# Output projection's second half tile by tile, with h kept in full for the FFN's combinations

## The chip, the cores and the metric

The kernel runs on one core of a Trainium2 chip. A time is the device time of one execution in microseconds (us). Five engines matter: TensorE (PE in the profile; PEld is its weight load, which overlaps it), VectorE (DVE), ScalarE (ACT), GpSimd (POOL), and SyncE (SP), whose queue issues most of the DMA transfers. Each engine takes its instructions in a fixed order; what waits at the head of an engine's or a queue's order holds all that stands behind it.

## The reference, cut to what matters

One decoder layer on x (1024 tokens by 1024 channels, float32): two attention branches are merged by gates, and then

```python
x = x + merged @ w_out                       # output projection
h2 = rms_norm(x, norm_ffn_g)
gu = h2 @ w_ffn_in                           # 1024 x 5632
x = x + (silu(gu[:, :2816]) * gu[:, 2816:]) @ w_ffn_down
return rms_norm(x, norm_final_g)
```

The change lies in the output projection, the norm behind it, and the first two of the 22 column blocks of the FFN's first product.

## The kernel before

**Precision.** Float32 products are made of three reduced ones. `split` (lines 98 to 100) turns a float32 tile into a high part, which ACT writes, and a low part, the difference, which DVE writes behind it. `mm3` (lines 102 to 105) then adds hi*hi, hi*lo and lo*hi into one PSUM bank: three matmuls for each block of 128 in the contraction, with names `wh` and `wl` for the two parts of a weight and `hT_t` for the two parts of the transposed activations.

**Buffers.** `load_w` (lines 110 to 129) brings a weight into one of two raw buffers `wr`, and splits it into one of two `wh`, `wl` pairs. The next load into a raw buffer is issued by SP when the splits have read it; the next split waits until PE has used the old pair. In the output projection the third and fourth quarter of the weight use pairs `wo` of their own, but the same two raw buffers. PSUM has six banks `pd` for products and two banks `pf`/`pt` for transposes and some products.

**The output projection** (lines 987 to 1027) goes over two halves of the 1024 output columns (`c0`). In each half, for the first 512 tokens (`hh == 0`, four tiles of 128 tokens) the contraction is the outer loop: for each of the eight blocks `k` all four tiles add three matmuls, 12 in all, and the weight quarters come in one by one. For the other four tiles (`hh == 1`) the tile is the outer loop: 24 matmuls a tile. Behind a tile, `take(t)` (lines 995 to 1000) adds the residual x on DVE. In the second half it also stores the row and calls `norm_transpose` (lines 167 to 180): ACT squares and sums the row, ACT and DVE make the scale, DVE writes the normed row `hn`, PE transposes it in two groups of four 128x128 blocks into the two banks `pt`, and `split` brings each bank to `hT_t`. With the contraction outside, the first four tiles of the second half end together.

**Beside it**, `right_side` (lines 976 to 985) loads two rows of blocks of `w_ffn_down` (1 MB) into one of three buffers `r`, makes four differences on POOL and stores them; eight of these run in the output projection, two in its first half.

**The seam to the FFN.** Two column blocks of the FFN are made plainly (`plain(0)`, `plain(1)`, lines 1049 to 1079), the others by a scheme with seven products for eight (`up`), which needs sums and differences of blocks of h2: T2, T3, T4 and T1. Between `plain(0)` and `plain(1)`, `back` adds hi and lo again to get each of the four blocks of h2 in float32 (four additions of 128x2048 on DVE), four more such operations make the combinations, and three splits write T3, T2 and T4.

**What sets the order.** A scheduler builds the order of each engine from the program with its own idea of durations; `tc.issue_after(i)` tells it to put an instruction behind i.

Of the kernel before, what the change touches and what calls it, by code (L numbers as in the profile page):

```python
# [15 lines left out]
P = 128  # L16
# [31 lines left out]
def layer_kernel(  # L48
# [49 lines left out]
    def split(hi, lo, src):  # L98
        last_hi[0] = nc.scalar.activation(out=hi, in_=src, func=AF.Copy)  # L99
        return nc.vector.tensor_tensor(out=lo, in0=src, in1=hi.bitcast(F32), op=ALU.subtract)  # L100
# [6 lines left out]
    last_mm, last_hi, last_sq = [None], [None], [None]  # L107
# [59 lines left out]
    def norm_transpose(xt, gain, hT, col, pool, by_sqrt, bufs=2):  # L167
# [7 lines left out]
        for k0 in range(0, KT, 4):  # L175
            pt = psf.tile([P, HALF], F32, tag="f", name=nm("pt"))
            for k in range(4):
                nc.tensor.transpose(pt[:, k * P:(k + 1) * P], hn[:, (k0 + k) * P:(k0 + k + 1) * P],
                                    ident[:])
# [790 lines left out]
    x1_dram = dpool.tile([NT, P, D], F32, name="x1_dram")  # L970
    x_ctx = pool_of("xpool", 1, side="right")
    x1 = x_ctx.__enter__().tile([P, NT, D], F32, name="x1")
    with pool_of("wout", 2) as mpool:
        gain2 = load_gain(mpool, norm_ffn_g)

        def right_side(n):
# [3 lines left out]
            nc.sync.dma_start(out=r[:].rearrange("p n b c -> p n (b c)"),  # L980
# [5 lines left out]

        for c0 in range(0, D, HALF):
            ws = []
            for hh in range(2):
# [5 lines left out]
                def take(t):  # L995
                    xs = x1[:, 4 * hh + t, c0:c0 + HALF]
                    nc.vector.tensor_tensor(out=xs, in0=pts[t][:], in1=xs, op=ALU.add)
                    if c0 > 0:
                        nc.scalar.dma_start(out=x1_dram[4 * hh + t], in_=x1[:, 4 * hh + t, :])
                        norm_transpose(x1[:, 4 * hh + t, :], gain2, hT[hh], t * P, mpool, True, 4)  # L1000

                if hh == 0:
                    for k in range(KT):
                        if k % 2 == 0:
                            src = w_out[k * P:(k + 2) * P, c0:c0 + HALF]
                            ws.append(load_w(src, 2, HALF) if k < 4 else
                                      load_w(src, 2, HALF, tag="wo", pool=mpool))
                            if c0 == 0:
                                with tc.issue_after(last_w[0].ins):
                                    last_w[0] = nc.sync.dma_start(  # L1010
                                        out=x1[:, k:k + 2, :], in_=x[k * P:(k + 2) * P, :].rearrange(
                                            "(t p) d -> p t d", p=P))
# [12 lines left out]
    x_ctx.__exit__(None, None, None)  # L1025


# [12 lines left out]
    k_ctx = pool_of("keep", 1, side="right")  # L1040
    f1 = k_ctx.__enter__().tile([P, 4, HALF], F32, name="f1")

    r_ctx = pool_of("odd", 2, side="right")
    rpool = r_ctx.__enter__()
# [4 lines left out]
    with pool_of("first", 2) as fpool:  # L1049

        def plain(j):
            sg = [fpool.tile([P, HALF], F32, tag="sg", name=nm("sg")) for _ in range(2)]
            a = fpool.tile([P, S], F32, tag="a", name=nm("a"))

            def evac_g(hh, pt):

                nc.scalar.activation(out=sg[hh][:], in_=pt[:], func=AF.Sigmoid)
# [308 lines left out]
```

## Time and profile before

| | |
|---|---|
| median of 3 runs | 1461.54 us (1459.87 to 1465.85) |
| the profiled execution | 1464.02 us, of which 1462.3 us are the profile's span |
| PE busy | 1439.0 us, 98% of the span |
| DVE, ACT, POOL busy | 956.4, 554.3, 505.1 us |
| output projection | about 707 to 797 us of the span |
| `plain(0)` and `plain(1)` | about 797 to 854 us |

A row of a timeline has the start, the length, the engine, the line, the operation with output and inputs, how many are merged into the row, and in brackets the idle time before it with what ended it. PE's lengths overlap, since matmuls are pipelined: its pace is read from start to start. A row of the table of windows has, for each engine, the busy us and the number of instructions, then the granted TensorE clock (PEclk), the busy share of the DMA engines, and GB/s.

### The profile page before, as it was taken

To read this page: it belongs to the slowest core of one execution; us is meant where nothing else is said; L and a number is where in the kernel's file an instruction comes from. 1 tells how busy PE (TensorE), PEld (TensorE's weight loads), DVE (VectorE), ACT (ScalarE), POOL (GpSimd) and SP (SyncE) were. 2 spreads that over 40 slices of the span, in tenths; PEclk is the share of its full clock that TensorE was granted. 3 is DMA by queue.
4 is the path that set the end of the run, shared out by engine and by line. 5 is a ranking of instruction groups with operands and counts; after the bars stand their busy time and mean duration, and the time that the engine had idled before them with its cause. 6 is when DMAs were issued, how large, how long until landed. Compare 5 with 4: busy or idle time off the path is not lost.

```text
span 1462.3 us, 18377 instructions
## 1 busy us (share of the span) xinstructions
PE 1439.0 (98%) x6876; PEld 1165.4 (80%) x6876; DVE 956.4 (65%) x1336; ACT 554.3 (38%) x824; POOL 505.1 (35%) x438
## 2 busy tenths in 40 slices
PE   8999999999999999999999999999999999999997
PEld 8898888877676776788887778888888888888886
DVE  6484654358889899936627874556665655765655
ACT  5333332236655523354315242322332223644333
POOL 1020444535533321110146176566666664100000
PEclk9999999999999999999999999999999999999999
DMA  8232454574543461275859322233332332966512
GB/s 232 73 101 79 145 165 122 138 215 125 135 115 110 152 223 37 73 236 162 306 201 336 122 75 72 90 105 108 108 109 97 105 115 101 353 252 231 186 47 85
DMA packets 165784, 213.58 MB, mean 146 GB/s; under 512 B 13760, under 2 KB 115136, under 8 KB 165440
## 3 DMA queue, kind: packets, MB, share of 16 engines
q1 hardware_dynamic: 129376, 119.06, 26.1%
q0 software_dynamic: 15344, 55.59, 10.7%
q10 hardware_dynamic: 20976, 37.76, 8.2%
q8 instruction: 54, 0.88, 0.2%
q14 instruction: 34, 0.28, 0.1%
HBM read 146.32 MB, written 66.06 MB: 145 GB/s over the span
## 4 chain that ended last, share of the span: by engine, by line
PE 87%; DVE 7%; issue 2%; POOL 2%; ACT 1%; DMA 1%; SPq 0%; ACTq 0%; DVEq 0%; POOLq 0%
PE pd L299 30%; PE pd L1281 10%; PE pf L299 7%; PE pd L103 7%; PE pd L104 6%; PE pd L105 6%; PE pf L104 3%; PE pf L105 3%; PE pf L103 3%; PE pd L711 1%; PE pd L197 1%; PE pd L200 1%; PE pd L196 1%; PE pd L660 1%; PE pd L661 1%
## 5 line engine op out<-in xcount | busy, mean ns | idle before, releaser
L299 PE MATMUL pd<-tT,wh 128*128 128x512 f32 x768 | 235.2, 389 | 0.7 <-ACT wh L99 0.6
L100 DVE TENSOR_TENSOR wl<-wr,wh 128x1024 fp32r<-128x1024 f32 (+2 forms) x110 | 132.3, 1204 | 129.3 <-ACT wh L99 128.6
L99 ACT ACTIVATE wh<-wr 128x1024 fp32r<-128x1024 f32 (+2 forms) x110 | 95.4, 867 | 282.0 <-PE pd L299 162.3
L299 PEld LDWEIGHTS pd<-tT,wh 128*128 128x128 f32 x768 | 143.9, 188 | 31.7 <-ACT wh L99 1.0
L299 PE MATMUL pd<-hT_t,wh 128*128 128x512 f32 x536 | 165.4, 389 | 0.0
L299 PE MATMUL pd<-tT,wl 128*128 128x512 f32 x384 | 147.6, 389 | 0.0
L299 PEld LDWEIGHTS pd<-hT_t,wh 128*128 128x128 f32 x536 | 100.5, 188 | 21.1 <-ACT cc L325 0.2
L105 PE MATMUL pf<-hT_t,wl 128*128 128x512 f32 x288 | 114.3, 397 | 0.0
L103 PE MATMUL pf<-hT_t,wh 128*128 128x512 f32 x288 | 113.8, 395 | 0.0
L104 PE MATMUL pf<-hT_t,wh 128*128 128x512 f32 x288 | 113.5, 394 | 0.0
L99 ACT ACTIVATE wh<-s 128x1024 fp32r<-128x1024 f32 x58 | 61.4, 1061 | 118.5 <-POOL s L286 91.7
L299 PE MATMUL pd<-hT_t,wl 128*128 128x512 f32 x268 | 104.3, 389 | 0.0
L285 POOL TENSOR_TENSOR s<-wr 128x512 f32<-128x512 f32 x29 | 60.4, 2084 | 125.9 <-DMA wr<-in_w_in_dram 71.1
L99 ACT ACTIVATE oh<-raw 128x1024 fp32r<-128x1024 f32 x66 | 70.0, 1062 | 81.0 <-PE pd L1281 31.4
L299 PE MATMUL pf<-hT_t,wh 128*128 128x512 f32 x320 | 98.7, 389 | 0.0
L100 DVE TENSOR_TENSOR wl<-s,wh 128x1024 fp32r<-128x1024 f32 x58 | 72.2, 1246 | 32.4 <-ACT wh L99 32.4
L1281 PE MATMUL pd<-ol,oh 128*128 128x512 f32 x224 | 87.1, 389 | 0.0
L1281 PE MATMUL pd<-oh,ol 128*128 128x512 f32 x224 | 86.5, 389 | 0.0
L984 POOL TENSOR_TENSOR r<-r 128x512 f32<-128x512 f32 x32 | 44.6, 1404 | 121.0 <-DMA r<-in_w_ffn_down_dram 119.7
L1281 PE MATMUL pd<-oh 128*128 128x512 f32 x224 | 84.4, 389 | 0.0
L299 PEld LDWEIGHTS pd<-tT,wl 128*128 128x128 f32 x384 | 72.1, 188 | 15.0
L100 DVE TENSOR_TENSOR ol<-raw,oh 128x1024 fp32r<-128x1024 f32 x66 | 76.5, 1220 | 6.4 <-ACT oh L99 5.8
(281 smaller groups left out, 3275.8 us busy)
## 6 DMA issues: line engine op xcount, KB each, us to landing
wr<-in_w_in_dram SPq DMA_DIRECT2D x46, 512.0 KB, 4.7
wr<-in_w_ffn_in_dram SPq DMA_DIRECT2D x44, 512.0 KB, 3.8
raw<-left_dram SPq DMA_DIRECT2D x56, 256.0 KB, 5.4
g_dram<-fst ACTq DMA_DIRECT2D x32, 256.0 KB, 2.3
land<-g_dram SPq DMA_DIRECT2D x16, 512.0 KB, 3.4
r<-in_w_ffn_down_dram SPq DMA_DIRECT2D x8, 1024.0 KB, 11.3
right_dram<-r POOLq DMA_DIRECT2D x8, 1024.0 KB, 7.3
left_dram<-f POOLq DMA_DIRECT2D x8, 1024.0 KB, 4.9
```

The source lines that it names most:

```text
L99: last_hi[0] = nc.scalar.activation(out=hi, in_=src, func=AF.Copy)
L100: return nc.vector.tensor_tensor(out=lo, in0=src, in1=hi.bitcast(F32), op=ALU.subtract)
L103: nc.tensor.matmul(psum, w.hi, m.hi, start=start, stop=False)
L104: nc.tensor.matmul(psum, w.hi, m.lo, start=False, stop=False)
L105: last_mm[0] = nc.tensor.matmul(psum, w.lo, m.hi, start=False, stop=stop)
L196: nc.tensor.matmul(pt[hh][:], w.hi[:, k], m.hi, start=(k == 0), stop=False)
L197: nc.tensor.matmul(pt[hh][:], w.hi[:, k], m.lo, start=False, stop=False)
L200: nc.tensor.matmul(pt[hh][:], w.lo[:, k], m.hi, start=False, stop=(k == kt - 1))
L285: nc.gpsimd.tensor_tensor(out=s12[:, :4], in0=u1, in1=u2, op=ALU.add)
L299: last_mm[0] = nc.tensor.matmul(bank[:], p, q, start=first and k == 0 and n == 0, stop=k == 3 and n == 2, skip_group_check=True)
L984: nc.gpsimd.tensor_tensor(out=out, in0=p, in1=q, op=ALU.subtract)
L1281: nc.tensor.matmul(bank[:], p, q, start=new and n == 0 and i == 0, stop=n == last and i == 2, skip_group_check=True)
```

## The change

The second half of the output projection is made tile by tile for all eight tiles; an ordering rule keeps each tile's matmuls behind those of the tile before. All four weight quarters of the second half are therefore loaded ahead of its first tile. Three `right_side` loads, instead of two, stand in the first half, two are told between the second half's weights, and three behind them. The rows x1 are four tiles instead of one, loaded in the order 0, 1, 2 and, later, 3.

Behind each transpose bank, ACT writes a third copy, h2 in full float32 (`also`), into f1 and f3 (first 512 tokens) or f2 and f4 (the other 512; these two are the places of x1[0] and x1[1], whose rows are done by then). The four additions `back` go. The first four of the last six groups of transposes are told a place among the matmuls of `plain(0)`'s gate (before its blocks 2, 4, 6 and 7), the last two among those of its up part (before 2 and 4). The gate weight of `plain(1)` is loaded ahead of the T2 split, and the places of buffers are moved so that the first raw weights of `up` need not wait for f1 to f4.

```diff
-    def norm_transpose(xt, gain, hT, col, pool, by_sqrt, bufs=2):
+    def norm_transpose(xt, gain, hT, col, pool, by_sqrt, bufs=2, also=None):
...
+            transposes.append(turned.ins)
             p4 = pt[:].rearrange("p (k t) -> p k t", k=4)
             split(hT.hi[:, k0:k0 + 4, col:col + P], hT.lo[:, k0:k0 + 4, col:col + P], p4)
+            if also:
+                nc.scalar.activation(out=also[k0 // 4][:, :, col:col + P], in_=p4, func=AF.Copy)
...
-    def projT1(w, h2, evac, hh):
+    def projT1(w, h2, evac, hh, behind={}):
         pt = pd()
         for k in range(KT):
-            mm3(pt[:], w[:, k], h2[hh][:, k], k == 0, k == KT - 1)
+            with tc.issue_after(behind[k]) if k in behind else ExitStack():
+                mm3(pt[:], w[:, k], h2[hh][:, k], k == 0, k == KT - 1)
         evac(hh, pt)
...
-    x1 = x_ctx.__enter__().tile([P, NT, D], F32, name="x1")
+    xpool = x_ctx.__enter__()
+    f3 = xpool.tile([P, 4, HALF], F32, name="f3")
+    x1 = {n: xpool.tile([P, 2, D], F32, name=nm("x1")) for n in (3, 0, 1, 2)}
+    f2, f4 = [x1[n][:].rearrange("p t (k c) -> p (t k) c", k=2) for n in range(2)]
+    blocks = [(f1[:], f3[:]), (f2, f4)]
...
+            def load_out(k):
+                src = w_out[k * P:(k + 2) * P, c0:c0 + HALF]
+                ws.append(load_w(src, 2, HALF) if k < 4 else load_w(src, 2, HALF, tag="wo", pool=mpool))
...
-                if hh == 0:
+                if hh == 0 and c0 == 0:
                     for k in range(KT):
                         if k % 2 == 0:
-                            src = w_out[k * P:(k + 2) * P, c0:c0 + HALF]
...
+                            load_out(k)
+                            if k < 6:
                                 with tc.issue_after(last_w[0].ins):
...
+                                    x_rows(k // 2)
                         for t in range(4):
                             mms(t, k)
-                    for n in range(2) if c0 == 0 else range(2, len(TWO_ROWS)):
-                        with tc.issue_after(last_w[0].ins):
-                            right_side(n)
+                    sides(0, 3)
+                    with tc.issue_after(last_w[0].ins):
+                        x_rows(3)
                     for t in range(4):
                         take(t)
-                else:
-                    for t in range(4):
-                        for k in range(KT):
+                    continue
+                if hh == 0:
+                    for k in range(0, KT, 2):
+                        load_out(k)
+                        if k == 2:
+                            sides(3, 5)
+                    sides(5, len(TWO_ROWS))
+                for t in range(4):
+                    for k in range(KT):
+                        with tc.issue_after(last_mm[0].ins) if k == 0 else ExitStack():
                             mms(t, k)
-                        take(t)
+                    take(t)
...
-        plain(0)
-        back(f3, B11)
-        back(f2, B12)
-        back(f4, B22)
-        vec(f1, f2, f3)
+        plain(0, weight(0))
+        vec(f1[:], f2, f1[:])
         vec(f2, f4, f2)
-        split(T3.hi, T3.lo, f2[:])
-        vec(f4, f4, f1)
-        split(T2.hi, T2.lo, f4[:])
-        back(f3, B21)
-        vec(f3, f3, f4)
+        split(T3.hi, T3.lo, f2)
+        vec(f4, f4, f1[:])
+        wg = weight((PLAIN - 1) * P)
+        with tc.issue_after(last_hi[0].ins), tc.issue_after(last_lo[0].ins):
+            split(T2.hi, T2.lo, f4)
+            vec(f3[:], f3[:], f4)
         split(T4.hi, T4.lo, f3[:])
```

**PE at the start of the second half.** Before (names: `pd_866` to `pd_869` are the four tiles of `hh == 0`, `pd_924` the first of `hh == 1`, `wh_870` the first weight quarter, `wh_873` the second, `wh_876` the third):

```order
L105 MATMUL pd_865_6168<-wh_857_6116,hT_t_91 128x512
L103 MATMUL pd_866_6269<-wh_870_6273,hT_t_91 128x512
L103 MATMUL pd_867_6270<-wh_870_6273,hT_t_91 128x512
L103 MATMUL pd_868_6271<-wh_870_6273,hT_t_91 128x512
L103 MATMUL pd_869_6272<-wh_870_6273,hT_t_91 128x512
...
L105 MATMUL pd_869_6272<-wh_873_6303,hT_t_91 128x512
L103 MATMUL pd_866_6269<-wh_876_6333,hT_t_91 128x512
```

Now (`pd_871` is the first tile, `pd_872` the second; quarters `wh_875`, `wh_878`, `wh_883`, `wh_886`, the low part of the third is `wl_884`, of the fourth `wl_887`):

```order
L104 MATMUL pd_871_6284<-wh_875_6288,hT_t_91 128x512
...
L104 MATMUL pd_871_6284<-wh_878_6294,hT_t_91 128x512
...
L104 MATMUL pd_871_6284<-wh_883_6314,hT_t_91 128x512
L105 MATMUL pd_871_6284<-wl_884_6315,hT_t_91 128x512
...
L104 MATMUL pd_871_6284<-wh_886_6320,hT_t_91 128x512
L105 MATMUL pd_871_6284<-wl_887_6321,hT_t_91 128x512
...
L104 MATMUL pd_872_6285<-wh_875_6288,hT_t_91 128x512
```

Between the first matmul of the half and the first that reads the third quarter stood 49 matmuls; now it is 12, and 18 to the fourth.

**SP's queue at the same place** (`wr` are raw weights, `r` the loads of `right_side`, `x` rows of x). Before:

```order
L980 DMA r_861_6154<-in_w_ffn_down_dram 128x2x1024
L122 DMA wr_872_6275<-in_w_out_dram 128x2x512
L122 DMA wr_875_6305<-in_w_out_dram 128x2x512
L122 DMA wr_878_6335<-in_w_out_dram 128x2x512
L122 DMA wr_881_6365<-in_w_out_dram 128x2x512
L980 DMA r_882_6393<-in_w_ffn_down_dram 128x2x1024
```

Now:

```order
L997 DMA r_866_6168<-in_w_ffn_down_dram 128x2x1024
L988 DMA x1_843_6018<-in_x_dram 128x2x1024
L123 DMA wr_877_6290<-in_w_out_dram 128x2x512
L123 DMA wr_880_6296<-in_w_out_dram 128x2x512
L997 DMA r_881_6300<-in_w_ffn_down_dram 128x2x1024
L123 DMA wr_885_6316<-in_w_out_dram 128x2x512
L123 DMA wr_888_6322<-in_w_out_dram 128x2x512
L997 DMA r_882_6307<-in_w_ffn_down_dram 128x2x1024
```

A load of `right_side` now stands ahead of the third and fourth quarter's loads; it reuses the buffer of the first such load, whose results must have been stored.

**PE in `plain(0)`** (`pd_976`/`pd_977` the gate and up bank, `pt` a transpose bank, `hn` a normed row). Before, the last four groups stand in one row:

```order
L178 MATMUL pt_945_6666<-ident_83,hn_937_6644 128x128 x4
L104 MATMUL pd_977_6845<-hT_t_91,wh_973_6812 128x512
L105 MATMUL pd_977_6845<-hT_t_91,wl_974_6813 128x512
L178 MATMUL pt_953_6714<-ident_83,hn_946_6699 128x128 x4
L178 MATMUL pt_954_6721<-ident_83,hn_946_6699 128x128 x4
L178 MATMUL pt_962_6769<-ident_83,hn_955_6754 128x128 x4
L178 MATMUL pt_963_6776<-ident_83,hn_955_6754 128x128 x4
L103 MATMUL pd_978_6871<-hT_t_91,wh_970_6806 128x512
```

Now three to ten matmuls stand between them:

```order
L181 MATMUL pt_957_6734<-ident_83,hn_950_6719 128x128 x4
L104 MATMUL pd_976_6830<-hT_t_91,wh_969_6817 128x512
L105 MATMUL pd_976_6830<-hT_t_91,wh_969_6817 128x512
L106 MATMUL pd_976_6830<-hT_t_91,wl_970_6818 128x512
L181 MATMUL pt_958_6742<-ident_83,hn_950_6719 128x128 x4
...
L106 MATMUL pd_976_6830<-hT_t_91,wl_970_6818 128x512
L181 MATMUL pt_966_6791<-ident_83,hn_959_6776 128x128 x4
```

`pt_966` is the first group of the last tile; it comes 30 matmuls behind the end of the output projection.

More of the change, by code (lines that the diff above doesn't have):

```diff
@@ L970, in layer_kernel, with x_rows @@
     x1_dram = dpool.tile([NT, P, D], F32, name="x1_dram")
+    k_ctx = pool_of("keep", 1, side="right")
+    f1 = k_ctx.__enter__().tile([P, 4, HALF], F32, name="f1")
     x_ctx = pool_of("xpool", 1, side="right")
-    x1 = x_ctx.__enter__().tile([P, NT, D], F32, name="x1")
+    xpool = x_ctx.__enter__()
[3 more added lines that the diff above has]
+    blocks = [(f1[:], f3[:]), (f2, f4)]
+    def x_rows(n):
+        last_w[0] = nc.sync.dma_start(out=x1[n][:], in_=x[2 * n * P:2 * (n + 1) * P, :].rearrange("(t p) d -> p t d", p=P))
     with pool_of("wout", 2) as mpool:
@@ L985, in right_side, with sides @@
             nc.gpsimd.dma_start(out=rows_of(right_dram[n]), in_=r[:].rearrange("p n b c -> p (n b) c"))
+        def sides(a, b):
+            for n in range(a, b):
+                with tc.issue_after(last_w[0].ins):
+                    right_side(n)
         for c0 in range(0, D, HALF):
             ws = []
+            def load_out(k):
+                src = w_out[k * P:(k + 2) * P, c0:c0 + HALF]
+                ws.append(load_w(src, 2, HALF) if k < 4 else load_w(src, 2, HALF, tag="wo", pool=mpool))
             for hh in range(2):
@@ L1039, in layer_kernel @@
     PLAIN = 2
[L1040 to L1044, printed above, removed]
     def raws(j):
@@ L1049, in layer_kernel, with weight, plain @@
     with pool_of("first", 2) as fpool:
[L1051 to L1053 removed]
+        reserve(fpool, ("pad", [3 * S], F32, 1))
+        def weight(c):
+            return load_w(w_ffn_in[:, c:c + P], KT, P)
+        def plain(j, wg):
+            a = fpool.tile([P, S], F32, tag="a", name=nm("a"), bufs=2)
+            sg = [a[:, hh * HALF:(hh + 1) * HALF] for hh in range(2)]
             def evac_g(hh, pt):
[L1057 to L1058 removed]
+                nc.scalar.activation(out=sg[hh], in_=pt[:], func=AF.Sigmoid)
+                nc.vector.tensor_tensor(out=sg[hh], in0=pt[:], in1=sg[hh], op=ALU.mult)
             def evac_u(hh, pt):
[L1061 to L1064 removed]
+                nc.vector.tensor_tensor(out=sg[hh], in0=pt[:], in1=sg[hh], op=ALU.mult)
+            wu = weight(DFF + j * P)
             if j == PLAIN - 1:
@@ L1079, in plain, with vec @@
             return odd
-        f2, f3, f4 = [fpool.tile([P, 4, HALF], F32, name=nm("f"), bufs=1) for _ in range(3)]
-        def vec(out, p, q, op=ALU.subtract):
-            nc.vector.tensor_tensor(out=out[:], in0=p[:], in1=q[:], op=op)
-        def back(out, b):
-            vec(out, b.hi.bitcast(F32), b.lo.bitcast(F32), ALU.add)
-        plain(0)
-        back(f3, B11)
-        back(f2, B12)
-        back(f4, B22)
-        vec(f1, f2, f3)
-        vec(f2, f4, f2)
-        split(T3.hi, T3.lo, f2[:])
-        vec(f4, f4, f1)
-        split(T2.hi, T2.lo, f4[:])
-        back(f3, B21)
-        vec(f3, f3, f4)
+        def vec(out, p, q):
+            return nc.vector.tensor_tensor(out=out, in0=p, in1=q, op=ALU.subtract)
+        plain(0, weight(0))
+        vec(f1[:], f2, f1[:])
+        vec(f2, f4, f2)
+        split(T3.hi, T3.lo, f2)
[4 more added lines that the diff above has]
+            vec(f3[:], f3[:], f4)
         split(T4.hi, T4.lo, f3[:])
-        for j in range(1, PLAIN):
-            odd = plain(j)
+        x_ctx.__exit__(None, None, None)
+        r_ctx = pool_of("odd", 2, side="right")
+        rpool = r_ctx.__enter__()
+        odd = plain(PLAIN - 1, wg)
         split(T1.hi, T1.lo, f1[:])
```

35 lines of the change are left out of this document (14 added, 21 removed).

## The prediction

> **What bounds the kernel now.** I read the page first, for what is busy, then PE's waits, then a table of windows along the stage that the change touches, and timelines at its gaps.
>
> ```profile
> span 1462.3 us, 18377 instructions
> PE 1439.0 (98%) x6876; PEld 1165.4 (80%) x6876; DVE 956.4 (65%) x1336; ACT 554.3 (38%) x824; POOL 505.1 (35%) x438
> ```
>
> PE is busy nearly always, and the order shows as many PE rows before as now. The change can only win what PE loses at its places. Between 790 and 870 us, PE's view of waits has
>
> ```profile
> PE pt L178 <- DVE hT_t L100: 3.6, 4, 2.3
> PE pd L200 <- DVE wl L100: 1.1, 1, 1.1
> PE pd L299 <- ACT wh L99: 0.6, 1, 0.6
> ```
>
> and the table of windows, cut at these gaps:
>
> ```profile
> 751.30:797.30 46.00, 46.00 (x217) 38.31 (x215) 24.82 (x52) 17.13 (x30) 26.01 (x22) 1.00 0.91 324
> 797.30:805.00 7.70, 5.29 (x21) 3.83 (x20) 7.58 (x12) 3.79 (x9) 7.15 (x6) 0.78 1.06 375
> 815.60:819.50 3.90, 2.63 (x19) 1.82 (x18) 2.47 (x4) 2.29 (x4) 0.00 (x0) 1.00 0.16 65
> 831.00:834.20 3.20, 2.08 (x9) 1.09 (x8) 3.20 (x3) 0.44 (x1) 0.00 (x0) 1.00 0.00 0
> 856.30:858.00 1.70, 1.09 (x6) 0.58 (x5) 1.12 (x2) 1.70 (x3) 1.60 (x1) 1.00 0.60 240
> 868.80:870.00 1.20, 1.10 (x5) 0.58 (x5) 0.49 (x1) 0.00 (x0) 1.12 (x2) 1.00 1.07 321
> ```
>
> The second half of the output projection (first row) has no gap. The seam behind it has five: PE idles 2.41, 1.27, 1.12, 0.61 and 0.10 us in the other rows (length less PE busy), 5.5 us in all. In the first of them DVE is busy 7.58 of 7.70 us: transposes wait for a bank that DVE has not emptied.
>
> A gap costs more than its length. PE's steady pace is the distance of these starts, 5 steps in 1.14 us, **0.227 us** a matmul; a lone group of four transposes costs 809.38 - 808.71 - 0.227 = 0.44 us:
>
> ```profile
> 747.64 0.39 PE L105 MATMUL pd<-wh,hT_t 128*128 128x512 f32 x1
> 748.78 0.39 PE L104 MATMUL pd<-wl,hT_t 128*128 128x512 f32 x1
> ...
> 808.71 0.60 PE L178 MATMUL pt<-ident,hn 128*128 128x128 f32 x4
> 809.07 0.48 PE L104 MATMUL pd<-hT_t,wh 128*128 128x512 f32 x1
> 809.38 0.40 PE L105 MATMUL pd<-hT_t,wl 128*128 128x512 f32 x1
> ```
>
> And the granted clock falls to half for 3.4 us behind stretches in which PE idled enough:
>
> ```profile
> 548.80:552.20 3.40, 2.10 (x14) 1.21 (x11) 3.40 (x9) 2.24 (x5) 0.71 (x1) 1.00 0.01 2
> 552.20:555.60 3.40, 3.40 (x9) 2.71 (x9) 3.40 (x7) 1.66 (x2) 0.00 (x0) 0.50 0.00 0
> ...
> 797.90:801.40 3.50, 1.33 (x9) 0.91 (x9) 3.45 (x7) 0.81 (x2) 3.34 (x3) 1.00 1.03 389
> 801.40:804.80 3.40, 3.40 (x10) 2.78 (x11) 3.33 (x6) 2.42 (x5) 3.00 (x4) 0.50 1.09 350
> ```
>
> A stretch of 3.4 us that was 62% busy (2.10 of 3.40) was followed by one at 0.50, which loses half of it, **1.7 us**. So the seam loses 5.5 idle + 1.7 clock + 1.8 of slow restarts = **9.0 us**, all there is to win. The 1.8 is an estimate, 0.35 for each of five gaps, from eight transposes behind the first gap and eight undisturbed (1.26 against 1.03) and one more slow matmul:
>
> ```profile
> 782.10 1.03 PE L178 MATMUL pt<-ident,hn 128*128 128x128 f32 x8
> ...
> 799.99 1.26 PE L178 MATMUL pt<-ident,hn 128*128 128x128 f32 x8 [2.32 <-DVE hT_t L100]
> ```
>
> **The change part by part.**
>
> *The seam's gaps.* The first four tiles ended together (the first row below); tile by tile one ends each 24 x 0.227 + 2 x 0.44 = 6.3 us. A tile then needs of ACT
>
> ```profile
> 771.42 2.73 DVE L997 TENSOR_TENSOR x<-pd,x 128x512 f32<-128x512 f32 x4 [11.51 <-PE pd L105]
> ...
> 809.35 0.60 ACT L99 ACTIVATE hT_t<-pt 128x512 fp32r<-128x512 f32 x1 [5.14 <-PE pt L178]
> ...
> 776.22 1.04 ACT L171 ACTIVATE hn<-x 128x1024 f32<-128x1024 f32 x1
> ```
>
> 1.04 for the square, about 0.5 of small ones, 2 x 0.60 for the high parts, and now 2 x 0.60 for the full copies (same size, same source; not in the trace, priced by this row): 3.9 of 6.3 us. Of DVE it needs
>
> ```profile
> 809.98 0.69 DVE L100 TENSOR_TENSOR hT_t<-pt,hT_t 128x512 fp32r<-128x512 f32 x1 [1.10 <-ACT hT_t L99]
> 787.08 1.28 DVE L173 SCALAR_TENSOR_TENSOR hn<-x,r,gain 128x1024 f32<-128x1024 f32 x1
> 806.79 2.09 DVE L173 SCALAR_TENSOR_TENSOR hn<-x,r,gain 128x1024 f32<-128x1024 f32 x1
> 827.51 2.28 DVE L1084 TENSOR_TENSOR f<-hT_t 128x2048 f32<-128x2048 f32 x1
> ...
> 842.81 6.55 POOL L285 TENSOR_TENSOR s<-wr 128x512 f32<-128x512 f32 x1 [31.71 <-DVE tT L100]
> ```
>
> 0.69 for the residual, 1.28 for hn (2.09 while POOL works), about 1 of small ones, 2 x 0.69: 4.3 to 5.2. Both fit, and the order puts a tile's transposes two tiles later, so they find their row ready: the first wait (2.41 us, then the half clock) goes. The four groups in one row (the second gap) now stand 3 to 10 matmuls apart. The third gap, the low part of `plain(1)`'s weight, stood behind `back`: four operations of 2.28 us leave DVE, 9.1 us, and that weight's split is moved ahead of two of the combinations. The fourth was POOL's sum for the first `up`, which began at 842.8; the raw weight that it needs is issued when DVE has split `plain(1)`'s second weight, some 10 us earlier now, and the new places of the buffers keep f1 to f4 off it. I take all five as gone: **-9.0**; bounds -9.0 and, if DVE or ACT falls behind once, -4.
>
> *One wait stays in the seam.* A transpose bank is now freed by three evacuations, and ACT's run in order. The last tile's first group is due 30 x 0.227 + 4 x 0.44 = 8.6 us behind the projection's end; the bank it needs was filled at about 6.5 us, and ACT has two high parts and two copies in between (4 x 0.60, less what PE's own steps hide): free at about 9.2. **+0.6**, bounds 0 and 3 (3 if ACT is another two copies and a square behind).
>
> *The first tile of the second half.* Here the change takes cover away. The raw buffer of the third weight quarter comes free when DVE has split the first; the first can be split only when PE has left the old pair. All this is the same in both kernels, up to the landing:
>
> ```profile
> 749.79 0.37 SPq L122 DMA_DIRECT2D wr<-in_w_out_dram  x1
> 751.15 0.37 SPq L122 DMA_DIRECT2D wr<-in_w_out_dram  x1
> 754.05 1.06 ACT L99 ACTIVATE wh<-wr 128x1024 fp32r<-128x1024 f32 x1 [4.18 <-DMA wr<-in_w_out_dram]
> 757.58 1.06 ACT L99 ACTIVATE wh<-wr 128x1024 fp32r<-128x1024 f32 x1 [2.48 <-DMA wr<-in_w_out_dram]
> 755.14 1.23 DVE L100 TENSOR_TENSOR wl<-wr,wh 128x1024 fp32r<-128x1024 f32 x1 [2.98 <-ACT wh L99]
> 758.68 1.23 DVE L100 TENSOR_TENSOR wl<-wr,wh 128x1024 fp32r<-128x1024 f32 x1 [2.31 <-ACT wh L99]
> ```
>
> The third quarter is split at 755.1 (high) and 756.4 (low), the fourth at 758.6 and 759.9. The half starts at 751.3. Before, the third was needed 49 matmuls later, at 762.4: hidden. Now it is 12, at 754.0, and the fourth at 755.4. PE waits for each in turn; after the fourth's low part at 759.9 five matmuls remain, so the tile ends at 761.1 instead of 751.3 + 24 x 0.227 = 756.7: **+4.4**. No other matmul can fill this: PE's rows of the first tile stand together. The fourth landed 6.4 us after its issue beside three loads of `right_side` issued right behind it, the third 4.2 us beside fewer. With the fourth at 4.2 too, it is split at 757.6 and the wait is 2.2: lower bound 2. The load of `right_side` that now stands ahead of the third quarter on SP waits for a store that POOL issues after seven differences instead of four:
>
> ```profile
> 727.85 5.29 POOL L984 TENSOR_TENSOR r<-r 128x512 f32<-128x512 f32 x4
> 733.08 0.95 POOL L985 DMA_DIRECT2D right_dram<-r  x1
> ...
> DMA to landing us min/median/max: 2.9/5.5/12.8
> ```
>
> At 1.32 us each, three more make the store start at 737 and land at 743 by the median, 750 at the slowest, when SP is due at 749.8. I take no delay; upper bound 7.
>
> In these 7 us PE is busy at most half, less than the 62% above, so the clock halves for one stretch: **+1.7**, bounds 0 and 3.4. The Trainium skill (page "TensorE: Matmul & The Clock Gate", section "Why this matters for your kernels") puts it otherwise: it warns of idle gaps over some 3 us and has the clock fall after a whole idle window. The gaps here are about 1 us each, so by that rule this term would be 0. The trace disagrees: the stretch from 548.8 on was 62% busy, and the clock fell.
>
> *Priced at nothing.* The later loads of x compete with the first half's fourth weight quarter, which landed at about 720 and is needed at 707.6 + 72 x 0.227 = 723.9; up to 2 if seven transfers halve its pace. POOL's differences only come earlier; beside them hn takes 2.09 instead of 1.28, which the 5.2 of 6.3 us above holds.
>
> **Sum**, on the profiled execution: 1462.3 - 9.0 + 0.6 + 4.4 + 1.7 = 1460.0 us of span, -2.3. That execution took 1464.02 with what lies around the span, 2.5 above the median of the runs; on the median it is 1461.5 - 2.3 = **1459.2**.
>
> **Rivals.**
>
> *A small price at the first tile.* The fourth quarter lands as fast as the third, and the clock holds: 1461.5 - 9.0 + 0.6 + 2.2 = 1455.3, down to 1452.5 if nothing waits at all. For it: DMA is less crowded, two loads of `right_side` instead of three behind the fourth quarter. Against: the third quarter alone forces 2 us, and it is bound by buffers that the change leaves alone. That the clock alone holds gives 1459.2 - 1.7 = 1457.5; I give it 0.10, inside the forecast's share, since it fell after 2.10 of 3.40 us. This is what the Trainium skill's rule on idle gaps (the page above) would bring.
>
> *The load ahead on SP comes late (slower side).* Place: SP's queue before the third quarter. Each us that the first store lands past 749.8 delays both quarters by one; from 752.1 on the kernel is slower than before. At 756 it is 1461.5 - 2.3 + 6.2 = 1465.4. For it: stores took up to 12.8 us, and POOL slows beside DVE. Against: the DMA engines are nearly idle in 740 to 750.
>
> *ACT becomes what transposes wait for, and the seam wins nothing.* In-order copies hold squares and high parts back; the seam keeps half its 9.0: 1461.5 - 4.5 + 0.6 + 6.1 = 1463.7; if all, 1468. For it: 16 more ACT operations in the stage and a third reader per bank. Against: 3.9 of 6.3 us.
>
> **How the numbers follow.** Forecast 0.60, small price 0.17, late load 0.11, ACT 0.12. The forecast's own range is 1456.5 to 1462; the range over all cases goes from 1453, near the first rival's end, to 1466, the late load. What a measurement tells from no change is about 0.5%, 7.3 us: faster means below 1454.2, slower above 1468.8. Faster holds most of the first rival's lower part and a little of an overestimated price: 0.16. Slower: the ends of the two bad rivals and what I do not see, 0.08. The rest, 0.76, is within.
>
> **What would show it.** Right: PE waits at the start of the second half for ACT's and DVE's `wh` and `wl`, some 4 us in four pieces, a PEclk of 0.5 for a stretch there; no wait of `pt` for DVE beyond 1 us; none for `wl` before `plain(1)` or `wh` before `up`. Wrong: no wait at the first tile, or a first tile late by more than 7 us, or waits of `pt` that only moved. It would also be wrong if PE's matmul rows outside the stage changed pace.

## The result and the profile after

The changed kernel takes 1467.62 us (median of 11 runs, 1465.02 to 1469.23) against 1461.57 us before (11 runs). The ratio is 1.0038 with a 95% interval of 1.0029 to 1.0047: **slower by 5.6 us** by the ratio (6.1 between the medians), less than the 7.3 us that the prediction took as the least that can be told from no change, but resolved by this interval. The forecast was 1459.2 us, faster by 2.3, and the range ended at 1466.

The profiled execution took 1467.87 us with a span of 1466.2; the page's head and its first row of engines:

```profile
span 1466.2 us, 18397 instructions
PE 1439.0 (98%) x6876; PEld 1165.2 (79%) x6876; DVE 945.9 (65%) x1332; ACT 562.7 (38%) x840; POOL 493.0 (34%) x438
```

PE's busy time is what it was (1439.0), DVE lost its additions (956.4 to 945.9) and ACT took on copies (554.3 to 562.7). So the 3.9 us of span are idle PE or a lower clock, and PE's view of waits between 690 and 900 us says where:

```profile
PE pd L104 <- ACT wh L99: 4.5, 1, 4.5
PE pd L306 <- ACT wh L99: 2.8, 1, 2.8
PE pt L181 <- ACT x L187: 0.5, 1, 0.5
PE pd L105 <- DVE wl L100: 0.5, 1, 0.5
```

The six waits of before (3.6, 1.1 and 0.6 us, in the three rows that the prediction shows) are gone. In their place stand two at the first tile of the second half (L104, L105), one of half a microsecond in the seam (`pt`), and one that no part of the prediction has: 2.8 us in `prod` (L306), at the first `up`.

**The first tile.** PE's timeline there:

```profile
753.21 0.39 PE L106 MATMUL pd<-wh,hT_t 128*128 128x512 f32 x1
758.10 0.79 PE L104 MATMUL pd<-wh,hT_t 128*128 128x512 f32 x1 [4.50 <-ACT wh L99]
759.36 0.79 PE L105 MATMUL pd<-wl,hT_t 128*128 128x512 f32 x1 [0.47 <-DVE wl L100]
759.96 0.63 PE L106 MATMUL pd<-wh,hT_t 128*128 128x512 f32 x1
...
762.79 0.40 PE L104 MATMUL pd<-wh,hT_t 128*128 128x512 f32 x1
```

The last row is ten matmuls behind the first: 9.58 us where 10 x 0.227 = 2.27 are due, so **7.3 us** are lost. ACT's and SP's timelines show the two late quarters:

```profile
749.23 1.73 SPq L123 DMA_DIRECT2D wr<-in_w_out_dram  x2
```

```profile
757.00 1.06 ACT L99 ACTIVATE wh<-wr 128x1024 fp32r<-128x1024 f32 x1 [7.69 <-DMA wr<-in_w_out_dram]
758.33 1.06 ACT L99 ACTIVATE wh<-wr 128x1024 fp32r<-128x1024 f32 x1 [0.27 <-DMA wr<-in_w_out_dram]
```

Both were issued from 749.23 on, half a microsecond earlier than before. The third landed at 757.0 instead of 754.0, the fourth at 758.3. The DMA engines were crowded; windows of after, then of before (the last two numbers are the DMA share and GB/s):

```profile
748.00:752.00 4.00, 4.00 (x19) 3.33 (x18) 3.12 (x3) 1.06 (x1) 1.73 (x2) 1.00 0.97 375
```

```profile
748.00:752.00 4.00, 4.00 (x20) 3.30 (x19) 2.98 (x3) 1.56 (x2) 0.00 (x0) 1.00 0.25 70
```

**The first `up`.** PE, ACT, SP and POOL at the new wait:

```profile
855.70 0.39 PE L306 MATMUL pd<-hT_t,wl 128*128 128x512 f32 x1
858.87 1.22 PE L306 MATMUL pd<-tT,wh 128*128 128x512 f32 x2 [2.78 <-ACT wh L99]
859.89 1.05 PE L306 MATMUL pf<-hT_t,wh 128*128 128x512 f32 x2
...
865.24 0.40 PE L306 MATMUL pd<-hT_t,wl 128*128 128x512 f32 x1
```

```profile
857.24 0.63 ACT L99 ACTIVATE wh<-wr 128x512 fp32r<-128x512 f32 x1 [7.36 <-DMA a_dram<-a]
857.77 1.04 ACT L99 ACTIVATE wh<-s 128x1024 fp32r<-128x1024 f32 x1
```

```profile
854.50 0.34 SPq L1103 DMA_DIRECT2D a_dram<-a  x1
```

```profile
843.34 2.27 POOL L293 TENSOR_TENSOR s<-s,wr 128x512 f32<-128x512 f32 x1
```

In the kernel before, the same sum ended at 856.2:

```profile
854.92 1.31 POOL L286 TENSOR_TENSOR s<-s,wr 128x512 f32<-128x512 f32 x1
```

The last PE row above is 16 matmuls behind the first: 9.54 us for 16 x 0.227 = 3.63, so **5.9 us** are lost. PE waits for the high part of S12 (`wh<-s`), whose sum POOL had finished at 845.6 (843.34 + 2.27). ACT took it 12 us later because the row ahead of it, the high part of A22 (`wh<-wr`, 128x512), waited 7.36 us for a store, `a_dram<-a`, which SP issued at 854.50. A22's place is why. In `up` the buffers are laid out as

```python
reserve(fpool, ("s", [KT, P], F32, 2), *[("s34" + n, [KT, P], F32R, 1) for n in "hl"],
        *[("a22" + n, [4, P], F32R, 1) for n in "hl"], ...
```

that is 8 KB of `s`, 4 and 4 KB of S34, then A22 from 16 KB on; in the pool before it, at the same start, a pad of `3 * S` floats (12 KB) and two `a` of 4 KB. The second `a`, `plain(1)`'s, begins at 16 KB too: A22 lies on it and may not be written until `plain(1)`'s result, made at the very end, is stored.

**The seam** did what the forecast said. Windows of after:

```profile
797.30:805.00 7.70, 7.70 (x40) 6.41 (x39) 5.35 (x12) 5.87 (x13) 0.00 (x0) 1.00 0.19 75
815.00:835.50 20.50, 20.03 (x93) 16.66 (x93) 18.42 (x14) 13.23 (x14) 0.00 (x0) 1.00 0.09 26
```

The first gap is closed and the clock full; of the rest only 0.47 us of idle is left.

### The profile page after: what moved, and what is told of

It reads as the page before. It is cut to its first block, busy times and chain, and to the rows that moved or that the text cites. A ratio compares the mean times of both kernels' runs of the same rounds, so it can differ in the third digit from the quotient of the medians.

```text
span 1466.2 us, 18397 instructions
## 1 busy us (share of the span) xinstructions
PE 1439.0 (98%) x6876; PEld 1165.2 (79%) x6876; DVE 945.9 (65%) x1332; ACT 562.7 (38%) x840; POOL 493.0 (34%) x438
## 3 DMA queue, kind: packets, MB, share of 16 engines
q0 software_dynamic: 15344, 55.59, 10.6%
## 4 chain that ended last, share of the span: by engine, by line
PE 89%; DVE 6%; issue 1%; DMA 1%; ACT 1%; POOL 1%; SPq 1%; ACTq 0%; POOLq 0%; DVEq 0%
PE pd L306 30%; PE pd L1300 10%; PE pf L306 7%; PE pd L105 6%; PE pd L106 6%; PE pd L104 6%; PE pf L106 3%; PE pf L105 3%; PE pf L104 3%; PE pd L203 2%; PE pd L204 2%; PE pd L207 2%; PE pd L718 1%; PE pd L667 1%; PE pd L668 1%
## 5 line engine op out<-in xcount | busy, mean ns | idle before, releaser
L306 PE MATMUL pd<-tT,wh 128*128 128x512 f32 x768 | 235.5, 390 | 2.8 <-ACT wh L99 2.8
L306 PEld LDWEIGHTS pd<-tT,wh 128*128 128x128 f32 x768 | 144.2, 188 | 33.2 <-ACT wh L99 3.2
L306 PE MATMUL pd<-hT_t,wh 128*128 128x512 f32 x536 | 167.0, 392 | 0.0
L306 PE MATMUL pd<-tT,wl 128*128 128x512 f32 x384 | 147.6, 389 | 0.0
L306 PEld LDWEIGHTS pd<-hT_t,wh 128*128 128x128 f32 x536 | 101.7, 190 | 21.6 <-ACT cc L332 0.2
L104 PE MATMUL pf<-hT_t,wh 128*128 128x512 f32 x288 | 113.6, 395 | 0.0
L105 PE MATMUL pf<-hT_t,wh 128*128 128x512 f32 x288 | 113.2, 393 | 0.0
L292 POOL TENSOR_TENSOR s<-wr 128x512 f32<-128x512 f32 x29 | 53.3, 1839 | 157.9 <-DMA wr<-in_w_in_dram 72.9
L306 PE MATMUL pd<-hT_t,wl 128*128 128x512 f32 x268 | 105.0, 392 | 0.0
L306 PE MATMUL pf<-hT_t,wh 128*128 128x512 f32 x320 | 99.1, 391 | 0.0
L104 PE MATMUL pd<-wh,hT_t 128*128 128x512 f32 (+1 forms) x208 | 77.7, 383 | 6.8 <-ACT wh L99 6.6
L306 PEld LDWEIGHTS pd<-tT,wl 128*128 128x128 f32 x384 | 72.1, 188 | 14.9
L105 PE MATMUL pd<-wl,hT_t 128*128 128x512 f32 (+1 forms) x208 | 80.0, 385 | 1.9 <-DVE wl L100 1.9
```

Of the source, the lines that this page charges most:

```text
L104: nc.tensor.matmul(psum, w.hi, m.hi, start=start, stop=False)
L105: nc.tensor.matmul(psum, w.hi, m.lo, start=False, stop=False)
L292: nc.gpsimd.tensor_tensor(out=s12[:, :4], in0=u1, in1=u2, op=ALU.add)
L306: last_mm[0] = nc.tensor.matmul(bank[:], p, q, start=first and k == 0 and n == 0, stop=k == 3 and n == 2, skip_group_check=True)
```

## The experiments

All were timed in five rounds beside the kernel before. The ratio is to it; 0.0010 is 1.5 us.

| run | what it is | median, us | ratio (95%) |
|---|---|---|---|
| changed | | 1467.62 | 1.0038 (1.0029 to 1.0047) |
| e1 | changed, pad of 2 | 1462.60 | 1.0010 (1.0001 to 1.0018) |
| e8 | changed, S12 ahead of A22 | 1465.53 | 1.0025 (1.0014 to 1.0036) |
| e2 | changed, `right_side` loads as before | 1467.14 | 1.0036 (1.0023 to 1.0049) |
| e3 | changed, own raw buffers | 1458.75 | 0.9983 (0.9975 to 0.9991) |
| e4 | pad of 2 and own raw buffers | 1455.19 | 0.9957 (0.9944 to 0.9970) |
| e5 | e1, contraction outside | 1464.34 | 1.0012 (1.0003 to 1.0021) |
| e6 | e4, order not told | 1458.47 | 0.9977 (0.9968 to 0.9986) |
| e7 | e4, no third copy | 1454.09 | 0.9947 (0.9933 to 0.9962) |
| e9 | e5, no third copy | 1456.34 | 0.9964 (0.9951 to 0.9976) |
| e10 | e7, order not told | 1455.17 | 0.9952 (0.9936 to 0.9968) |
| e11 | e9, order not told | 1459.56 | 0.9985 (0.9975 to 0.9996) |
| e12 | e7, weight of `plain(1)` behind T4 | 1454.00 | 0.9945 (0.9929 to 0.9962) |

### e1 and e8: the wait before `up`

e1 moves a place and leaves every engine's order as it is:

```diff
-        reserve(fpool, ("pad", [3 * S], F32, 1))
+        reserve(fpool, ("pad", [2 * S], F32, 1))
```

> The changed kernel with one number of its layout altered: the pad ahead of plain's two buffers `a` is 2 rows of S instead of 3, so that the second `a` lies where S34's low part comes later and no longer where the high part of the first `up`'s A22 comes. The order of every engine is the same. Theory (the store of plain(1)'s `a` must land before ACT can write A22's high part, and S12's high part stands behind that): PE's wait of 2.8 us at 856 and the half clock behind it go, 6.0 us in all, from 1467.6 to about 1461.7 us, level with the kernel before. Rival (ACT's wait there is for the weight or for POOL's sum, the store only lands at the same time): 1467 to 1468, the same wait. Rival (wait goes, clock stays half because of other idle time): about 1464.5.

Measured 1.0010: 0.0028, or 4.1 us, better than the changed kernel; the theory had 6.0. ACT, in e1, takes A22 and S12 without a wait as soon as T1's split is done:

```profile
852.46 0.61 ACT L99 ACTIVATE wh<-wr 128x512 fp32r<-128x512 f32 x1
852.97 1.05 ACT L99 ACTIVATE wh<-s 128x1024 fp32r<-128x1024 f32 x1
```

and PE has no wait at L306, nor a halved clock behind it, so the 5.9 us of that place are gone and the store is their cause. That the time fell by less is in part the first tile: in e1's profiled execution it cost 8.7 us instead of 7.3 (17 matmuls take 12.51 us from 754.51 on, where 3.86 are due), because both of its halved windows lay behind the wait, full of matmuls. Whether e1's other executions share this is not known.

e8 keeps the place and lets two rows change places on ACT and on DVE:

```diff
-            A1, S12, S34, A22 = left_side(fpool, *(odd if j == PLAIN + 1 else raws(j)), 2, 1)
+            A1, S12, S34, A22 = left_side(fpool, *(odd if j == PLAIN + 1 else raws(j)), 2, 1, j == PLAIN)
```

> The changed kernel with its pad of 3 kept, so that A22's high part still lies on plain(1)'s `a` and must wait for its store; only ACT and DVE now take S12's parts ahead of A22's in the first `up` (two rows change places on each). Theory (what cost 6.0 us is not the store as such but S12 queued behind it): the wait at 856 falls to 0.6 us or less and the clock holds, as in e1, 1462 to 1463. Rival (PE needs A22 itself soon, or the wait goes on to the operations behind A22 on ACT: c, the next weights): half of the gain or less, 1464.5 to 1467.

The theory as I put it for e8 fell, the rival held (1.0025; the 1.9 us that it is better than the changed kernel lie within the intervals). S12 comes in time (851.11), and the store now holds what is next behind A22, the copy `c` that frees a bank:

```profile
859.03 0.63 ACT L99 ACTIVATE wh<-wr 128x512 fp32r<-128x512 f32 x1 [6.88 <-DMA a_dram<-a]
859.56 0.58 ACT L1141 ACTIVATE c<-pd 128x512 f32<-128x512 f32 x1
```

```profile
857.70 0.61 PE L306 MATMUL pf<-hT_t,wh 128*128 128x512 f32 x2
860.20 1.12 PE L306 MATMUL pd<-hT_t,wh 128*128 128x512 f32 x2 [1.88 <-ACT c L1141]
```

Turning the queue passes the wait on; removing the cause removes it.

### e2, e3 and e4: the first tile

e2 puts the loads of `right_side` where they were before, e3 gives the late quarters raw buffers of their own:

```diff
-                    sides(0, 3)
+                    sides(0, 2)
...
-                        if k == 2:
-                            sides(3, 5)
-                    sides(5, len(TWO_ROWS))
+                    sides(2, len(TWO_ROWS))
```

```diff
-                ws.append(load_w(src, 2, HALF) if k < 4 else load_w(src, 2, HALF, tag="wo", pool=mpool))
+                ws.append(load_w(src, 2, HALF) if k < 4 else load_w(src, 2, HALF, tag="wo", pool=mpool, rpool=mpool if c0 else None))
```

> The changed kernel with the loads of right_side placed as in the kernel before: two in the first half, the other six behind all four weight quarters of the second half. Theory (in the changed kernel the third quarter is issued on time, at 749.2, but shares the DMA engines with a load and two stores of right_side and lands at 757.0 instead of 754.0): the third quarter lands at about 754 and the fourth by 757.5 or earlier, PE's wait at the first tile falls from 4.5 to about 1.5 us and a second one of 1 to 2 us comes for the fourth; with the clock still half for a stretch 1464 to 1465.5, with the clock held 1462 to 1463. Rival (the quarters land late whatever is beside them): 1467 to 1468.

> The changed kernel with raw buffers of their own for the third and fourth weight quarter of the second half, so that their loads need not wait until the first two are split. Theory (the first tile's wait is only the late third and fourth quarter, 4.5 + 0.5 us of idle, 0.9 of slow restarts and 1.4 of half clock, 7.3 us in all): about 1460.3. Their split must still wait until PE leaves the old pair, at about 750 and 751.3, which is 2 us ahead of the need: no wait at the first tile. Rival (PE then waits for DVE's low parts, four splits of 1.23 us in a row from 748): 1462 to 1464. Rival (the gain is given back in the seam, where ACT and DVE fall behind): 1465 or more.

In e2 the third quarter lands at 753.8, 3 us earlier, as the theory had it. The time does not move (1.0036). The fourth still lands at 757.8, and PE's timeline has four waits instead of two:

```profile
754.06 0.39 PE L106 MATMUL pd<-wh,hT_t 128*128 128x512 f32 x1
754.90 0.50 PE L104 MATMUL pd<-wh,hT_t 128*128 128x512 f32 x1 [0.45 <-ACT wh L99]
756.16 0.50 PE L105 MATMUL pd<-wl,hT_t 128*128 128x512 f32 x1 [0.76 <-DVE wl L100]
...
758.92 0.63 PE L104 MATMUL pd<-wh,hT_t 128*128 128x512 f32 x1 [1.34 <-ACT wh L99]
760.18 0.79 PE L105 MATMUL pd<-wl,hT_t 128*128 128x512 f32 x1 [0.63 <-DVE wl L100]
...
766.17 0.39 PE L104 MATMUL pd<-wh,hT_t 128*128 128x512 f32 x1
```

Less idle, 3.2 us against 5.0, but from the first row to the last, 22 matmuls on, are 12.1 us for 22 x 0.227 = 5.0: **7.1 lost**, as much as in the changed kernel. More matmuls ran at half the clock. This is the pattern of four waits that the forecast had drawn, and its price is the same as with a late third quarter.

In e3 PE has no wait there at all, and the kernel passes the one before (0.9983). The 0.0055 (8.0 us) agree with the 7.3 expected: each ratio is known to some 1.2 us. e4 has both edits:

> Both: the pad of 2 and the raw buffers of their own. Theory (the two waits are separate and are all that the change cost): 1467.6 - 6.0 - 7.3 = 1454.3, 0.5 % faster than the kernel before, so the seam's gain of 9 us less small change is there in full. Rival (one loss hides the other, or the seam itself lost): 1458 to 1462.

0.9957: 11.8 us better than the changed kernel, where e1 and e3 by themselves gave 4.1 and 8.0. The two losses are separate and add up. Against the kernel before the gain is 6.3 us (4.4 to 8.2), not the 9 of the expectation; more on this below. Of PE's waits from 690 to 900 us e4 keeps one row, the one that the prediction had left in the seam:

```profile
PE pt L181 <- ACT x L187: 0.5, 1, 0.5
```

### e5, e6, e7 and e9 to e12: what each part earns

e5, made from e1, undoes the order by tiles (with it, the loads of `right_side` in the second half go behind its four weight quarters, and the raw buffers stay shared). e6 and e7 are made from e4: e6 undoes the told order, e7 the third copy. The edits, cut to what matters:

```diff
-                if hh == 0 and c0 == 0:
+                if hh == 0:
...
-                if hh == 0:
-                    for k in range(0, KT, 2):
...
```

```diff
-                    projT1(wg, hT, evac_g, hh, dict(zip((2, 4, 6, 7), transposes[-6:-2])) if hh == 0 else {})
-                    projT1(wu, hT, evac_u, hh, dict(zip((2, 4), transposes[-2:])) if hh == 0 else {})
+                    projT1(wg, hT, evac_g, hh, {})
+                    projT1(wu, hT, evac_u, hh, {})
```

```diff
-                        norm_transpose(xt, gain2, hT[hh], t * P, mpool, True, 4, blocks[hh])
+                        norm_transpose(xt, gain2, hT[hh], t * P, mpool, True, 4)
...
         plain(0, weight(0))
+        for f, b in ((f1[:], B11), (f2, B12), (f4, B22)):
+            nc.vector.tensor_tensor(out=f, in0=b.hi.bitcast(F32), in1=b.lo.bitcast(F32), op=ALU.add)
...
+            nc.vector.tensor_tensor(out=f3[:], in0=B21.hi.bitcast(F32), in1=B21.lo.bitcast(F32), op=ALU.add)
             vec(f3[:], f3[:], f4)
```

> Tile by tile undone alone: the changed kernel with the pad of 2, and in the second half too the contraction is the outer loop for the first four tiles, as in the kernel before; the copies of h, the told order of the transposes and all else stay. From e1 (1462.6) the wait at the first tile goes, 7.3 us, to 1455.3. Theory (the order by tiles is what removes the first gap of the seam, 2.4 us idle, 1.7 of half clock and about 1 of slow restarts): that gap comes back, 1455.3 + 4 to 5 = about 1460. Rival (the copies and the told order remove that gap by themselves, since DVE is rid of the additions and PE of the crowded transposes): 1455 to 1456, and the order by tiles earned nothing of its own.

> e4 (pad of 2, raw buffers of their own, 1455.2) with the order of the last six groups of transposes left to the scheduler. Theory (the told order removed the second gap, where four groups stood in a row: 1.27 us idle and some 0.7 of restarts): 1457. Rival (the scheduler spreads them by itself, now that rows are ready earlier): 1455.2, no difference.

> e4 without the third copy that ACT makes of each transpose bank: the four additions of high and low part are back on DVE between plain(0) and plain(1), four times 2.28 us; the weight of plain(1) is still split ahead of T2. Theory (the third gap was DVE's additions ahead of that weight's low part, 1.12 us idle and 0.35 of restart, and it comes back since three additions still stand ahead): about 1456.7, and the wait of 0.5 us on ACT's copy goes, so 1456.2. Rival (moving the weight ahead was enough): 1454.7. Rival (the additions crowd DVE in the whole stage up to T1's split, and the first `up` waits): 1458 or more.

e5 fits neither number (1.0012, 1464.3): the seam's gap came back larger than it ever was, and for another engine:

```profile
PE pt L181 <- ACT f L187: 4.1, 1, 4.1
PE pt L181 <- ACT x L187: 2.1, 2, 1.6
```

These are waits for the third copy. ACT's timeline of e5 shows what held it:

```profile
797.14 1.06 ACT L174 ACTIVATE hn<-x 128x1024 f32<-128x1024 f32 x1
...
799.83 0.29 ACT L155 ACTIVATE t<-ss,epst 128x1 f32<-128x1 f32 x1 [1.53 <-DVE x L1025]
800.05 1.20 ACT L187 ACTIVATE f<-pt 128x512 f32<-128x512 f32 x2
```

The copies stand behind the next row's square and its scale; the scale's wait is put down to DVE. This is the prediction's rival on ACT, in a kernel where four rows become ready together. In e7, with the order by tiles and no copy at all, PE waits for nothing between 690 and 900 us. The time is 0.9947; the copies did not help (e4, 0.9957, intervals overlap). My theory for e7 fell. e6 gives 0.9977, 2.9 us worse than e4 (the intervals just touch), by the two rows

```profile
PE pt L181 <- ACT x L187: 1.6, 1, 1.6
PE pd L207 <- DVE wl L100: 1.5, 1, 1.5
```

so with the copies the told order is needed. Three more runs fill in the square. e9 is e5 with e7's edit, e10 and e11 are e7 and e9 with e6's:

> e5 without ACT's third copy of each transpose bank (the additions of high and low part are back on DVE), so the second half has the contraction outside for its first four tiles as in the kernel before; the told order, the weight ahead of T2 and the places of buffers stay. In e5 PE waited 4.1 and 1.6 us in the seam for ACT's copies. Theory (with the copies away the seam of the contraction-outside order waits for DVE as in the kernel before, 2 to 3 us and a half clock, since four rows become ready together): ratio to the kernel before 0.997 to 0.999, and the order by tiles earns 3 to 6 us (e7 0.9947). Rival (ACT's copies were all that made this order wait): 0.9945 to 0.9955, as e7, and the order by tiles earns nothing.

> e7 (0.9947 of the kernel before; tile by tile, raw buffers of their own, no third copy) with the order of the last six groups of transposes left to the scheduler. In e6, with the copies, that cost 1.6 us of wait for ACT's copy and 1.5 for a weight's low part, 3.3 us in all. Theory (the told order is worth something by itself, since the scheduler puts groups too close for two banks): 0.996 to 0.997. Rival (the told order only makes room for the copies): 0.9945 to 0.9952.

> e9 (contraction outside in the second half, no third copy, 0.9964 of the kernel before) with the order of the last six groups of transposes left to the scheduler. What is left of the change is the weight of plain(1) ahead of the T2 split, the places of buffers and the loads' places. Theory (in e9 the told order is what took the seam's first and second gap away, since without tile by tile the scheduler crowds the groups): PE waits for DVE's hT_t again, 3 us or more with a half clock, ratio 0.999 to 1.001. Rival (the two gaps went with the moved loads and weight): 0.996 to 0.997, as e9.

| ratio | copies, told | copies, untold | additions, told | additions, untold |
|---|---|---|---|---|
| by tiles, own raw buffers | 0.9957 | 0.9977 | 0.9947 | 0.9952 |
| contraction outside | 1.0012 | not run | 0.9964 | 0.9985 |

With the contraction outside, the copies cost 0.0048 (7.0 us, e5 and e9). The told order earns 0.0021 there (e9 and e11, intervals that just touch) and nothing that shows by tiles without copies (e7 and e10, whose rival held). The order by tiles earns 0.0033 untold (e10 and e11) and 0.0017 told, where the intervals overlap. The two rows of the table also differ in the raw buffers and in the places of the `right_side` loads; in the lower row PE waits for no weight, so this should matter little, but it was not tried apart. It seems that two of the edits work on one thing, the crowd of transposes behind the output projection: of the 0.0038 between e11 and e7 the told order alone takes about half, the order by tiles alone most. e9's theory, that the seam would wait without the order by tiles, held only in part: it waits for 0.7 us, not 2 to 3, with no half clock. e11's came true in kind (PE waits 2.6 us for DVE and 0.7 for ACT, and the clock is halved for one window) but hardly in size: 0.9985, between the two numbers, with an interval that reaches into the theory's. What of e11's remaining 2.2 us against before is the places, the weight moved ahead, or the loads, was not taken apart.

e12 puts the weight of `plain(1)` back behind T4's split, one more edit not yet tried:

```diff
-        wg = weight((PLAIN - 1) * P)
-        with tc.issue_after(last_hi[0].ins), tc.issue_after(last_lo[0].ins):
-            split(T2.hi, T2.lo, f4)
...
+        split(T2.hi, T2.lo, f4)
...
         split(T4.hi, T4.lo, f3[:])
+        wg = weight((PLAIN - 1) * P)
```

> e7 (0.9947) with the gate weight of plain(1) loaded behind the T4 split again, as in the kernel before, and the ordering rule on T2's split away. Theory (the weight ahead removed the third gap, 1.12 us idle and 0.35 of restart, and by it the fourth, 0.61 and 0.35): PE waits for wl before plain(1) and for wh before `up`, ratio 0.996 to 0.9965. Rival (the third gap went because the scheduler has DVE free earlier): 0.9945 to 0.9952.

The rival held: 0.9945, and in the window row PE is busy throughout.

```profile
790.00:870.00 80.00, 80.00 (x370) 66.27 (x369) 64.18 (x64) 32.00 (x40) 25.11 (x14) 1.00 0.35 107
```

DVE does all its additions in that stretch (64.18 us of 80) and nobody waits for them. e12 and e7 beat both kernels, the one before by 7 to 8 us (e12: 0.0055, 8.0 us, by the ratio; 1454.00 against 1461.39 by the medians).

## Why the prediction was wrong

The span was put at 1460.0 and is 1466.2, 6.2 us more. By the prediction's own steps:

**The fourth gap was the step that failed.** "The fourth was POOL's sum for the first `up` ... the new places of the buffers keep f1 to f4 off it. I take all five as gone." The first half is right: the sum was ready at 845.6, 10.6 us earlier than before (854.92 + 1.31 = 856.2). But I asked only what the moved places free, not what they now lie on. The new `a` of `plain(1)` came to lie under A22, and ACT's order put S12 behind A22. Priced at -0.6 to -1.0, it cost 5.9. e1 takes it away by one number of the layout. The list of signs at the prediction's end did name it ("none for `wh` before `up`"), but no rival had it, and the range had no room for it.

**The first tile was the right mechanism, 1.2 us too small.** Expected were 4.4 of wait and 1.7 of half clock, 6.1; measured 7.3. Of it, 5.7 us are the two waits with their slow restarts (4.89 + 1.26 us for two steps of 0.227), 1.6 the half clock behind them. The third quarter came 3 us late: the rival of "the load ahead on SP" named the stage but not the cause. SP issued both quarters on time; what was late was the landing, among the loads and stores of `right_side` that I had set aside with "the DMA engines are nearly idle in 740 to 750", a reading of the kernel before, and too kind even to that: there they were busy for 0.64 of 740 to 744. e2 shows that it hardly mattered, since the fourth quarter set the end either way. What made both late was the shared raw buffer (e3). By the prediction's own list a first tile late by more than 7 us speaks against it, and this one was (7.3).

**The seam was right in its waits.** 9.0 us were to go and 0.6 to stay; the waits went, and 0.47 us of idle with a restart of 0.2 stayed. Between the same two matmuls, the 3762nd and the 4303rd of PE (745 and 870 us before), lie 125.0 us before and 116.3 in e4: 8.7 less, where 8.4 were forecast. The copy's price by the evacuation's row (0.60) was 0.594, and ACT kept up (33.19 of 65.90 us from 790 on). e4 is the forecast's seam without the two losses. Its median is 1455.2, though, where the forecast would have had 1461.5 - 8.4 = 1453.1: the 9.0 us hold for the one execution of before that was profiled, with its halved window, and not for the median. And the reason was only half right: e7 and e12 show that DVE could have kept its additions and the weight its place. What they keep (the order by tiles, the told order, the places of buffers and loads) was enough.

**The clock term was right in size and wrong in length**: two halved windows instead of one, the first of them mostly idle. The size is luck in part. The threshold came from a stretch of smaller matmuls (64x128 and 64x256 in the trace) that was 62% busy; among 128x512 matmuls the clock held behind windows that were 53% busy (last section).

**The sum.** 5.9 and 1.2 make 7.1 us. The seam took back 0.3, and PE came to the second half 0.6 us earlier in the profiled execution of after (750.7 instead of 751.3), which leaves the 6.2.

**The rest** is the profiled execution. I took 2.5 us off for the profile of before, which stood above its median; the profile after stands 0.25 above its own. So 6.2 us of span became 8.4 on the median. The step from span to median is itself doubtful: the profiled execution of before had a mean granted clock of 0.993, and 19 of the 23 executions of before that ran beside e1 to e4 had 0.995 or more, with 1459.4 to 1462.0 us. So the median execution had probably not lost the 1.7 us of clock that I took off it. With one trace of the kernel before, this is not shown.

## What to carry to other kernels

When an edit moves buffers, ask of each new place what was there last and when that is done with: a store at the end of one stage, under a tile that an in-order engine writes early in the next, holds the whole queue (5.9 us here), and reordering that queue only passes the wait on (e8). An order that needs its inputs sooner needs the buffers that let them come sooner: tile by tile with shared raw buffers lost 7.3 us, with two of their own nothing. And when two edits aim at the same wait, undo each by itself; here the third copy, the told order and the order by tiles overlapped, and the copy was not needed.

## What the runs showed of the hardware

**How long a gap is was not what decided the clock.** The same wait of 2.78 us before `up` cost 5.9 us in the changed kernel and 3.1 in e3, by PE's starts (in e3 16 matmuls from 850.46 to 857.17). In these traces the granted clock changes only on a grid of 3.41 us; these are windows of that grid, of after, then of e3:

```profile
854.74:858.16 3.42, 1.35 (x6) 0.77 (x5) 0.26 (x1) 0.92 (x2) 0.00 (x0) 1.00 0.38 153
858.16:861.57 3.41, 2.70 (x6) 2.15 (x7) 2.95 (x3) 3.03 (x4) 1.28 (x2) 0.50 0.44 129
861.57:864.98 3.41, 3.41 (x9) 2.64 (x8) 3.38 (x3) 1.06 (x1) 2.25 (x2) 0.50 0.71 185
```

```profile
849.04:852.46 3.42, 1.81 (x8) 1.16 (x7) 0.19 (x1) 0.46 (x1) 0.00 (x0) 1.00 0.38 153
852.46:855.87 3.41, 2.24 (x10) 1.86 (x11) 2.74 (x3) 3.41 (x5) 0.90 (x1) 1.00 0.33 98
```

(In e3 the grid is counted from the clock's last change before, at 575.98 us, in steps of 3.4133.) In e3 the gap fell across a border of the grid, so that neither window was empty enough (1.81 and 2.24 us busy), and the clock held. In the changed kernel one window had 1.35, and the next two were halved; the first of these still had a gap (2.70 of 3.41), the second had none, and behind it the clock was full.

From 690 us to the last matmul, where nearly all matmuls are 128x512, the fourteen traces agree on where the border lies. At full clock, it fell behind every window with at most 1.64 us of PE busy (e2's first tile) and behind none with 1.80 or more (e6); at 1.75 us, about half a window, e11 has one of each. Of the halved windows, those with up to 2.92 us busy (e1) were followed by another, those with 3.23 or more (after) by a full one.

The Trainium skill (page "TensorE: Matmul & The Clock Gate", section "Why this matters for your kernels") warns of gaps over some 3 us; at e2's first tile no gap was longer than 1.34 us, and two windows were halved, while e2's wait of 2.79 us before `up` halved none. Here the traces differ from that rule.

Where the grid lies is not the kernel's doing. In the stage around 550 us, which no edit touches, the clock fell at 552.21 us in the kernel before, at 550.96 in after, at 571.89 in e1, and in e4 for two windows from 570.02 on. So a term of some 2.8 us, as between these two gaps, can differ between executions of one kernel, and a single profiled execution shows only one case. The five executions of e2 took 1465.74 us at a mean granted clock of 0.995 up to 1467.71 at 0.992.

**The same sum on POOL took 6.55 us or 1.28.** The first of the 128x512 sums took 6.55 us before, where DVE had no pause, and 1.28 in the changed kernel, where DVE stood still from 839.5 to 843.2:

```profile
840.83 1.28 POOL L292 TENSOR_TENSOR s<-wr 128x512 f32<-128x512 f32 x1 [49.92 <-DMA wr<-in_w_ffn_in_dram]
```

```profile
843.21 1.24 DVE L100 TENSOR_TENSOR wl<-wr,wh 128x1024 fp32r<-128x1024 f32 x1 [3.71 <-ACT wh L99]
```

DVE's next row then ran beside POOL's sum of 2.27 us (843.34, shown above). That DVE's work is the cause was not tested.
